# First mixer: the value projection moved from the end of the preceding head pair to the beginning of its own pair

## The chip, the core and the metric

The kernel runs on one core of a Trainium2 chip. Its engines have their own in-order queues and meet through semaphores: TensorE (PE) for matrix products and transposes, VectorE (DVE) and ScalarE (ACT) for elementwise work, GpSimd (POOL) and SyncE (SP), which here mostly issue transfers. The metric is the device time of one execution in microseconds; a smaller number is better.

## The reference

The reference is one step of a two-layer streaming encoder with model width 1024: a prompt of 1024 new frames and 8 running streams of 16 frames each, whose past of 1024 frames lies in caches. Layer 0 has a mixer with two halves, layer 1 a banded attention; each layer ends in an MLP. Only the first mixer matters here:

```
def ab_project(h, w_in):
    p = h @ w_in
    q, k, v, a, g = jnp.split(p, [...], axis=-1)
    return heads(q), heads(k), heads(v), a * jax.nn.sigmoid(g)

def stick_breaking(q, k, v, q_pos, k_pos):
    z = jnp.einsum('bqhd,bkhd->bhqk', q, k) * (HEAD_DIM ** -0.5)
    log_keep = jnp.where(mask, jax.nn.log_sigmoid(-z), 0.0)
    between = lax.cumsum(log_keep, axis=3, reverse=True) - log_keep
    w = jnp.where(mask, jnp.exp(jax.nn.log_sigmoid(z) + between), 0.0)
    return jnp.einsum('bhqk,bkhd->bqhd', w, v)

out = jnp.concatenate([a_out, c_out], axis=-1) @ w_out
```

There are 8 heads of 64, handled as four pairs of 128 columns. The other half of the mixer, `c_out`, is a causal depthwise convolution of width 31 over 512 channels of `a * sigmoid(g)`, followed by a layer norm and a SiLU. The new k and v of every head, and the last rows of the convolution's input, are outputs too.

## The kernel before, in words

**Tiles.** The 1024 prompt frames and the 8 x 16 sample frames form 1152 columns, in three groups of 384 (`G`, `NG`). A projection chunk makes 128 output columns of `w_in`: for each group it takes 24 matmuls of 128x384 (8 parts of the width, each as three products of the split halves), so 72 in all. These are `psp<-h,hl_wi`; in names such as `psp122` the digits are the head pair, the chunk (0 is q, 1 is k, 2 is v) and the group. `chunk_steps` makes the steps of a chunk, each step 12 matmuls.

**One head pair.** `expand_qk` copies q and k of the pair into the form that the score products take; half of it goes through transfers on POOL's queue (`k`, `l`). The scores `z` of a block of queries go to ACT (sigmoid) and DVE (the scan, `sg`), come back to PE for transposition (`tpa`) and for the product with the values (`ava`). The output goes as `cpa` to a DRAM tile, `cat_d`. The values take their own way: the third group is evacuated by ACT, the tile `sv` is written out by POOL, DVE then overwrites it in place with differences of neighbouring rows (`differences`), ACT negates the first column, and PE transposes it (`vt`, in `expand_v`). The differences overwrite what the write-out reads, so they wait for it to land. The running streams have steps of their own: key tiles `ct..k` come from the cache in blocks of 512 KB, three buffers in turn, and PE multiplies each with the queries (`zs`); then come `zn`, the softmax-like part, transposes (`st`, `sn`), products with cached values (`so`) and a last transposition (`sq`).

**The convolution.** Its 4 x 31 taps are pairs of DVE instructions (line 737) that have nothing to do with PE. `TAPS` says how many of the 124 are laid into the start and into head pairs 0, 1 and 2; what is left goes to pair 3. When a channel block has its last tap, its sum is put into `cat_d` (`cat_d<-u`), from where the layer norm (`conv_norm`: loads `yl`, mean product `mu`, ...) reads it in pair 3.

**Order.** Each piece of work is a `Step` with an estimated PE time, an estimated DVE time, a name, and optionally the name of a step it should follow and a lag. `merge` interleaves lists of steps so that each list progresses in proportion, and holds a step back until the modelled time of its predecessor plus the lag is over. `level` then spreads the taps by DVE time. The result is a fixed program order for all engines. In `mixer0` (lines 657 to 1018), before pair 0 all of chunk q, k and v of pair 0 are projected, with no other PE work between them. In pair p the lists are the attention steps with `expand_v` among the first, the stream's steps, the list `fill` with the projections for pair p + 1 (and, in pairs 0 and 1, the two chunks of the convolution's input for pair p + 2), and the taps. The weights of the chunks are loaded in a fixed sequence, each one chunk ahead, by SP.

**Pair 3** has no more projections. Its list `fill` holds the first half of the output projection instead: `ready_chunks` loads finished 128-column chunks of `cat_d` back (`cr`, on SP) and splits them into `cat`, and the products `psoa<-cat` follow. The tile of `cr` is that of `sk`, and one is in use at a time, so a chunk is loaded when the one before has been split.

Of the kernel before, what the change touches and what calls it, by code (L numbers as in the profile page):

```python
# [17 lines left out]
KC = 8  # L18
T = 1152
TP = 1024  # L20
TAPS = (26, 36, 38, 24)
G = 384
NG = 3
HD = 64
# [54 lines left out]
def level(steps, extra):  # L79


    pe, dve = sum(s.pe for s in steps), sum(s.dve for s in steps + extra)
    out, at, done, extra = [], 0.0, 0.0, list(extra)
    for s in steps:
        while extra and done + 0.5 * extra[0].dve < at / pe * dve:
            done += extra[0].dve
            out.append(extra.pop(0))
        out.append(s)
        at += s.pe
        done += s.dve  # L90
    return out + extra
# [7 lines left out]
def run(steps):  # L99
    for s in steps:  # L100
        s.go()
# [23 lines left out]
def tile_trunk(ctx, tc, ins, outs):  # L125
# [184 lines left out]
    def chunk_steps(n, got, ahead, h, ks, evac, name, depth=1, per=12):  # L310

        steps = [Step(0.0, lambda: [ahead(n + d) for d in range(depth + 1)], 1200.0)]
        for g in range(NG):
            box = {}

            def ps(g=g, box=box):
                if "p" not in box:
                    box["p"] = bank(f"ps{name}{g}")
                return box["p"]

            steps += dense(ps, lambda: got[n], h, g, ks, per)
            steps.append(Step(0.0, lambda g=g, ps=ps: evac(ps(), g), 470.0))
        return steps
# [333 lines left out]
    def mixer0():  # L657
        with ExitStack() as st:
# [8 lines left out]
            pp = Bufs(st.enter_context(pool("pair0")), ve=2)  # L667
# [77 lines left out]
            def ag(c):  # L745
                return (chunk_steps(at[16 + c], got, ahead, h, ks, lambda ps, g: gate(c, ps, g), f"g{c}")
                        + chunk_steps(at[12 + c], got, ahead, h, ks, lambda ps, g: value(c, ps, g), f"a{c}"))
# [121 lines left out]
                nc.vector.tensor_copy(unit, ident)  # L869


            def proj(p):
                steps = []
                for n, tag in enumerate(("sq", "sk", "sv")):
                    def evac(ps, g, n=n, tag=tag):
                        if g == 0:
                            S[tag, p] = pp.tile([P, T], F32, tag, f"{tag}0{p}")
                        if g < 2:
                            tt(S[tag, p][:, g * G:g * G + G], ps[:, :G], rstd[g], ALU.mult)
                        else:  # L880
                            ACT(S[tag, p][:, g * G:], ps[:, :G], AF.Copy)
                        if g == 2 and n:
                            put(outs["sb_k" if n == 1 else "sb_v"][p], S[tag, p])
                    steps += chunk_steps(at[4 * n + p], got, ahead, h, ks, evac, f"p{p}{n}")
                return steps

            def expand_qk(p):
                q, k = S["sq", p], S["sk", p]
                expand(qs, kd, kl, q, k)
                S["qn"] = pp.tile([P, P], F32, "qn", f"qn0{p}")  # L890
                S["kn"] = pp.tile([P, P], F32, "kn", f"kn0{p}")
                ACT(S["qn"], q[:, TP:], AF.Copy, scale=0.125)
                ACT(S["kn"], k[:, TP:], AF.Copy)
# [85 lines left out]
            start()  # L979
            qs, kd, kl = ([ep.tile([P, TP], F32R, f"{n}{i}", f"{n}{i}") for i in range(2)] for n in "qkl")  # L980
            vs = pp.tile([P, 8, 2, HD], F32, "vs", "vs0")
            run(level(proj(0), taps[:TAPS[0]]))
            taps = taps[TAPS[0]:]
            carry, cat_t = [], None
            for p in range(4):
                S["p"] = p
                expand_qk(p)
                if p < 3:
                    fill = proj(p + 1)
                    if p < 2:  # L990
                        fill[10:10] = ag(p + 2)
                    n = TAPS[p + 1]
                    mix, now, taps = [], taps[:n], taps[n:]
                else:
                    cat_t = new_hs("cat0")
                    (first, fill), now = part_out(0, range(3), pp, cat_t), []
                    for s in taps:
                        s.pe = 900.0
                    mix = taps + conv_norm(lambda: (conv_pool.close(), Bufs(st.enter_context(pool("ln")), t1=3, yl=5))[1],
                                           cat_t)  # L1000
                cat = Cat(0, p, wk, cat_t)
                jobs = attend(p, cat)
                body, left = pipeline(jobs[1:], jobs[0][2])
                steps = carry + [jobs[0][0]] + [Step(327.0, lambda p=p, g=g: expand_v(p, g)) for g in range(NG)]
                if p == 3:
                    late, = ready_chunks(0, [2], pp, cat_t)
                    late.name, late.after, late.lag = "ready", carry[-1].name, 3000.0
                    fill[0].after, fill[0].lag = "ready", 5000.0
                    fill = ready_chunks(0, range(2), pp, cat_t) + first + [late] + fill
                steps += [jobs[0][1]] + body  # L1010
                carry = left
                if p == 3:
                    steps += carry
                cs = sample_out(cat, wk, p)
                load = sample_caches(0, p, cp)
                sample = two_samples(*(sample_steps(0, p, bg, S, wk, load, soft, cs) for bg in range(2)))
                run(level(merge(steps, sample, fill, mix), now))
            return cat_t

# [68 lines left out]
    def part_out(layer, ks, pp, cat_t):  # L1088

        wo = ins["w_out_ab"] if layer == 0 else ins["w_out_c"]  # L1090
        got, ahead = weights_ahead([(wo[fc], ks) for fc in range(KC)], f"wo{layer}a")
        steps, xo = [], {}

        def old(fc):
            if fc < KC and fc not in xo:
                xo[fc] = pp.tile([P, T], F32, ("sq", "sv")[fc % 2], f"xo{layer}{fc}")
                if layer == 0:
                    dma(xo[fc].rearrange("p (g t) -> p g t", g=NG), ins["x"][:, :, fc, :].rearrange("g p t -> p g t"))
                else:
                    dma(xo[fc], x_d[:, fc, :])  # L1100

        for fc in range(KC):
            def evac(ps, g, fc=fc):
                xs = xo[fc][:, g * G:g * G + G]
                tt(xs, xs, ps[:, :G], ALU.add)
                if g == 2:
                    put(xm_d[layer][:, fc, :], xo[fc])
            steps.append(Step(0.0, lambda fc=fc: (old(fc), old(fc + 1))))
            steps += chunk_steps(fc, got, ahead, cat_t, ks, evac, f"oa{layer}{fc}", per=6)

        n = -(-len(SPLIT) * len(ks) // 6) + 1
        first = [steps[i] for i in (1, 2, 2 + n, 2 + 2 * n)]
        return first, [s for s in steps if s not in first]
# [872 lines left out]
```

## Time and profile before

| | |
|---|---|
| time, median of 3 runs | 2727.28 us (2727.0 to 2727.28) |
| the profiled execution | 2730.68 us |
| its span on the core | 2728.9 us |
| mean granted PE clock | 0.993 |
| PE busy | 2662.6 us, 98% |
| DVE busy | 2040.6 us, 75% |
| chunks before pair 0 (216 `psp` without a break) | 70.35 to 107.95 us |
| head pairs 0 to 2 | about 108 to 404 us |
| head pair 3 and its output projection | about 404 to 530 us |

A row of a timeline gives the start, the length of a run of like instructions on one engine, the line and operation, output<-inputs, the shape, the count, and in brackets the idle time of the engine ahead of it with what ended it. A row of windows gives, for a stretch of time, each engine's busy time with the number of instructions, then the granted PE clock, the DMA engines' busy share and the GB/s moved. A row of DMA issues gives output<-input, the issuing queue, the count, the size and the median us from issue to landing.

### The profile page before, as it was taken

The numbers are of one execution on the slowest core, as the hardware profiler recorded it, in microseconds if no ns is written. First come the engines' busy times: TensorE is split into PE (matmuls) and PEld (weight loads), VectorE is DVE, ScalarE is ACT, GpSimd is POOL, SyncE is SP. The second block draws the span as 40 slices with busy tenths as digits, with TensorE's granted clock in tenths as the row PEclk, the third lists the DMA queues.
The fourth block names the chain that finished last, engine by engine and source line by source line (L and its number), as shares of the span: only waits on it lengthen the run. The fifth ranks groups of instructions, "written<-read, shape, count | busy, mean of one in ns | idle before, by whom it ended". The sixth has DMA issues, their size and how long they took to land.

```text
span 2728.9 us, 50505 instructions
## 1 busy us (share of the span) xinstructions
PE 2662.6 (98%) x19362; PEld 2553.8 (94%) x19362; DVE 2040.6 (75%) x4105; ACT 1365.7 (50%) x2854; POOL 330.5 (12%) x599
## 2 busy tenths in 40 slices
PE   8999998999999999999999999998999999999998
PEld 8888886899999999999999999997999999999998
DVE  7999996787777755768577777778787777647577
ACT  5344456755555543445355555555455555534344
POOL 1000111131111100000011111110321111100001
PEclk9999999999999999999999999999999999999999
DMA  4344447443333486335444444446543334674344
GB/s 159 104 128 149 146 141 241 171 145 141 140 138 138 151 290 224 108 113 178 145 141 139 129 139 141 137 127 218 181 140 138 143 141 147 233 254 135 96 125 146
DMA packets 173203, 422.90 MB, mean 155 GB/s; under 512 B 25968, under 2 KB 53808, under 8 KB 170912
## 3 DMA queue, kind: packets, MB, share of 16 engines
q1 hardware_dynamic: 135696, 288.38, 32.6%
q0 software_dynamic: 37120, 131.27, 13.9%
q8 instruction: 152, 2.49, 0.4%
q14 instruction: 91, 0.75, 0.1%
q10 hardware_dynamic: 144, 0.02, 0.0%
HBM read 289.60 MB, written 117.34 MB: 149 GB/s over the span
## 4 chain that ended last, share of the span: by engine, by line
PE 84%; DVE 7%; ACT 3%; issue 3%; DMA 3%; POOL 0%; SPq 0%; DVEq 0%; ACTq 0%; POOLq 0%
PE pd L1705 26%; PE um L1480 25%; PE psc L225 10%; PE psp L225 4%; PE avc L469 2%; PE tpc L457 2%; PE psoa L225 2%; PE f L225 1%; PE zs L570 1%; PE zc L1220 1%; PE ava L398 1%; DVE y L737 1%; PE so L604 1%; PE psg L225 1%; PE psa L225 1%
## 5 line engine op out<-in xcount | busy, mean ns | idle before, releaser
L225 PE MATMUL psc<-h,hl_wc 128*128 128x384 f32 x1728 | 327.1, 339 | 0.0
L225 PEld LDWEIGHTS psc<-h,hl_wc 128*128 128x128 f32 x1728 | 296.8, 188 | 13.3 <-issue 10.9
L1480 PE MATMUL um<-sl,hl_m 128*128 128x288 f32 x1548 | 240.8, 296 | 0.0
L1480 PEld LDWEIGHTS um<-sl,hl_m 128*128 128x128 f32 x1548 | 218.2, 189 | 0.0
L1705 PE MATMUL pd<-tm,hl_wd 128*128 128x288 f32 x1584 | 214.7, 294 | 0.0
L1705 PEld LDWEIGHTS pd<-tm,hl_wd 128*128 128x128 f32 x1584 | 211.3, 189 | 0.0
L737 DVE SCALAR_TENSOR_TENSOR y<-u,dw,y 128x1024 f32<-128x1024 f32 (+1 forms) x232 | 177.5, 805 | 0.7
L1487 ACT ACTIVATE hdm<-hdm 128x288 f32<-128x288 f32 x192 | 84.7, 442 | 156.4 <-DVE hdm L1486 154.8
L225 PE MATMUL psp<-h,hl_wi 128*128 128x384 f32 x864 | 162.5, 340 | 0.0
L186 DVE TENSOR_TENSOR tm<-xr,tm 128x576 fp32r<-128x576 f32 (+1 forms) x120 | 85.7, 715 | 94.8 <-ACT tm L185 94.6
L225 PEld LDWEIGHTS psp<-h,hl_wi 128*128 128x128 f32 x864 | 148.4, 188 | 6.2 <-issue 5.1
L185 ACT ACTIVATE tm<-xr 128x576 fp32r<-128x576 f32 (+1 forms) x120 | 77.6, 647 | 94.7 <-PE pd L1705 75.9
L1480 PE MATMUL um<-sl,hl 128*128 128x288 f32 x756 | 119.1, 296 | 0.0
L1187 ACT ACTIVATE s<-s,mxc 128x640 f32<-128x640 f32 (+4 forms) x128 | 88.8, 694 | 60.2 <-DVE mxc L1184 58.6
L1705 PE MATMUL pd<-th,hl_wd 128*128 128x288 f32 x792 | 113.9, 297 | 3.8 <-DVE th L186 3.7
L1705 PEld LDWEIGHTS pd<-th,hl_wd 128*128 128x128 f32 x792 | 108.7, 191 | 4.5 <-DVE th L186 4.2
L1705 PE MATMUL pd<-xr,hl_wd 128*128 128x288 f32 x792 | 111.9, 295 | 0.0
L1705 PEld LDWEIGHTS pd<-xr,hl_wd 128*128 128x128 f32 x792 | 107.4, 189 | 0.0
L1480 PEld LDWEIGHTS um<-sl,hl 128*128 128x128 f32 x756 | 106.4, 188 | 0.8
L1705 PE MATMUL pd<-tm,hl 128*128 128x288 f32 x768 | 104.9, 295 | 0.0
L1705 PEld LDWEIGHTS pd<-tm,hl 128*128 128x128 f32 x768 | 103.1, 188 | 0.0
L185 ACT ACTIVATE whc<-tpc 128x512 fp32r<-128x512 f32 (+1 forms) x144 | 72.5, 523 | 46.7 <-PE tpc L457 45.7
(530 smaller groups left out, 6536.8 us busy)
## 6 DMA issues: line engine op xcount, KB each, us to landing
xr<-hb_d SPq DMA_DIRECT2D x208, 288.0 KB, 2.9
xr<-in_w_up_dram SPq DMA_DIRECT2D x64, 512.0 KB, 4.0
hb_d<-hdm POOLq DMA_DIRECT2D x96, 288.0 KB, 2.4
hb_d<-t POOLq DMA_DIRECT2D x96, 288.0 KB, 2.4
wm<-in_w_down_dram SPq DMA_DIRECT2D x64, 256.0 KB, 4.1
st_wd<-in_w_down_dram SPq DMA_DIRECT2D x64, 256.0 KB, 3.5
st_wc<-in_w_in_c_dram SPq DMA_DIRECT2D x44, 256.0 KB, 2.6
xm_d<-xo POOLq DMA_DIRECT2D x16, 576.0 KB, 3.8
```

The source lines that it names most:

```text
L185: ACT(hi, src, AF.Copy)
L186: return tt(lo, src, f(hi), ALU.subtract)
L225: mm(ps()[:, :G], hl[:, a, at:at + P], act[g][k // 4][b][:, k % 4, :], start=n == 0, stop=n == len(todo) - 1)
L398: mm(st["av"][64 * m:64 * m + 64, o0:o0 + n], vs[:, j, i], st["w"][gi][:, c0:c0 + n], start=gi == 0, stop=gi == last)
L457: nc.tensor.transpose(tp[:, c0 + q * P:c0 + (q + 1) * P], blocks.get(j, tile_q), ident)
L469: mm(st["av"][:, o0:o0 + n], vs[:, j, i].rearrange("p a d -> p (a d)"), src[:, c0:c0 + n], start=st["done"] == 0, stop=st["done"] == nmm - 1)
L570: mm(box["z"][at // 512][own, at % 512:at % 512 + kw], qb[:, own], k[:, b * kw:b * kw + kw], start=True, stop=True)
L737: stt(src if j == CW - 1 else dst, src, wj, dst, ALU.mult, ALU.add)
L1187: ACT(s[:, :n], s[:, :n], AF.Exp, bias=mx, scale=-1.0, accum_out=tot)
L1480: mm(banks[b, n][:, :TQ], w[:, a, c * P:c * P + P], combo(key, c)[:, h, n * TQ:n * TQ + TQ], start=k < 3 and c == 0 and i == 0, stop=c == ...
L1487: ACT(y, y, AF.Relu)
L1705: mm(ps, w[:, a, m * P:m * P + P], b[:, h, (n - ns[0]) * TQ:(n - ns[0]) * TQ + TQ], start=first and s == 0, stop=j == NJ - 1 and s == 2, s ...
```

## The change

Before pair 0 only q and k are projected. Each pair starts its `fill` with its own v, then projects q of the next pair, the convolution's input chunks (pairs 0 and 1) and k of the next pair. `expand_qk` becomes a step of its own, with lags behind it for the first score block and for the stream's queries; the transposes of v wait, in the model, for the end of the v chunk plus 3 us. In pair 3, v comes first in `fill`, then the two ready chunks and the output projection; the third chunk waits for the transposes of v. The taps are dealt 17, 40, 40, 27 where they were 26, 36, 38, 24. The sequence of the weight chunks does not change, nor does any instruction's work.

```diff
-TAPS = (26, 36, 38, 24)
+TAPS = (17, 40, 40, 27)
...
-            def proj(p):
+            def proj(p, *ns):
                 steps = []
-                for n, tag in enumerate(("sq", "sk", "sv")):
+                for n in ns:
+                    tag = ("sq", "sk", "sv")[n]
+
                     def evac(ps, g, n=n, tag=tag):
...
                     steps += chunk_steps(at[4 * n + p], got, ahead, h, ks, evac, f"p{p}{n}")
+                steps[-1].name = f"p{p}{ns[-1]}"
                 return steps
...
-            run(level(proj(0), taps[:TAPS[0]]))
+            run(level(proj(0, 0, 1), taps[:TAPS[0]]))
             taps = taps[TAPS[0]:]
             carry, cat_t = [], None
             for p in range(4):
                 S["p"] = p
-                expand_qk(p)
+                fill = proj(p, 2)
                 if p < 3:
-                    fill = proj(p + 1)
+                    fill += proj(p + 1, 0)
                     if p < 2:
-                        fill[10:10] = ag(p + 2)
+                        fill += ag(p + 2)
+                    fill += proj(p + 1, 1)
                     n = TAPS[p + 1]
                     mix, now, taps = [], taps[:n], taps[n:]
                 else:
                     cat_t = new_hs("cat0")
-                    (first, fill), now = part_out(0, range(3), pp, cat_t), []
+                    (first, later), now = part_out(0, range(3), pp, cat_t), []
...
                 body, left = pipeline(jobs[1:], jobs[0][2])
-                steps = carry + [jobs[0][0]] + [Step(327.0, lambda p=p, g=g: expand_v(p, g)) for g in range(NG)]
+                jobs[0][0].after, jobs[0][0].lag = f"x{p}", 6000.0
+                turned = [Step(327.0, lambda p=p, g=g: expand_v(p, g)) for g in range(NG)]
+                turned[0].after, turned[0].lag = f"p{p}2", 3000.0
+                turned[-1].name = f"v{p}"
+                steps = [Step(0.0, lambda p=p: expand_qk(p), 0.0, f"x{p}")] + carry + [*jobs[0][:2]] + turned + body
                 if p == 3:
                     late, = ready_chunks(0, [2], pp, cat_t)
-                    late.name, late.after, late.lag = "ready", carry[-1].name, 3000.0
-                    fill[0].after, fill[0].lag = "ready", 5000.0
-                    fill = ready_chunks(0, range(2), pp, cat_t) + first + [late] + fill
-                steps += [jobs[0][1]] + body
+                    late.name, late.after, late.lag = "ready", f"v{p}", 0.0
+                    later[0].after, later[0].lag = "ready", 5000.0
+                    fill += ready_chunks(0, range(2), pp, cat_t) + first + [late] + later
...
                 sample = two_samples(*(sample_steps(0, p, bg, S, wk, load, soft, cs) for bg in range(2)))
+                sample[0].after, sample[0].lag = f"x{p}", 8000.0
```

What this moves is seen in the program order. The first place is PE in pair 1, around the transposes of v (`vt010` to `vt012`). Before, the last v matmul (`psp122`) stands 78 rows ahead of the first transpose, with two groups of the next q between them:

```order
L225 MATMUL psp201_2310<-h0_71_191,hl_wi12_1_2015 128x384
L398 MATMUL ava013_2347<-wa0130_2234,vs0_747 64x256 x2
L398 MATMUL ava013_2347<-wa0131_2257,vs0_747 64x256 x2
L398 MATMUL ava013_2347<-wa0132_2264,vs0_747 64x256 x2
L398 MATMUL ava013_2347<-wa0133_2298,vs0_747 64x256
L398 MATMUL ava013_2347<-wa0133_2298,vs0_747 64x128
L943 MATMUL z1000_2366<-k0_743,q0_741 128x128
L944 MATMUL z1000_2366<-l0_745,q0_741 128x128
L946 MATMUL z1000_2366<-maskd_126,unit_127 128x128
L913 MATMUL vt010_2379<-ident_69,sv01_2071 128x128 x3
```

Now the last v matmul is followed by the 24 matmuls of one group of the next q (`psp200`) and then at once by the transposes. These are the last of the 24 and what follows:

```order
L225 MATMUL psp200_2340<-h0_61_187,hl_wi12_1_2122 128x384
L225 MATMUL psp200_2340<-h0_60_186,hl_wi12_1_2122 128x384
L225 MATMUL psp200_2340<-h0_71_191,hl_wi12_1_2122 128x384
L225 MATMUL psp200_2340<-h0_70_190,hl_wi12_1_2122 128x384
L916 MATMUL vt010_2374<-ident_69,sv01_2183 128x128 x3
L916 MATMUL vt011_2379<-ident_69,sv01_2183 128x128 x3
L916 MATMUL vt012_2386<-ident_69,sv01_2183 128x128 x3
L946 MATMUL z1020_2394<-k0_743,q0_741 128x384
```

In pair 0, 24 of these matmuls and four key tiles stand between (before: 24 matmuls), and in pair 2, 24 and three key tiles.

The second place is POOL's queue at the start of pair 3, ahead of the loads for the layer norm (`yl00` to `yl03`, which the products `mu` read). Before:

```order
L741 DMA cat_d0_109<-u3_2527 128x8x16
L883 DMA out_sb_v_dram<-sv03_4091 128x1152
L363 DMA cat_d0_109<-cs02_4012 128x128
L363 DMA cat_d0_109<-cpa212_4321 64x256
L352 DMA l1_746<-l1_746 64x1024
L1034 DMA yl00_4346<-cat_d0_109 128x384
L1034 DMA yl01_4347<-cat_d0_109 128x384
L1034 DMA yl02_4348<-cat_d0_109 128x384
L1034 DMA yl03_4349<-cat_d0_109 128x384
```

Now two more transfers of `expand_qk` stand between `cpa212` and the loads, and the write-out of v comes after them:

```order
L363 DMA cat_d0_109<-cpa212_4241 64x256
L352 DMA l0_745<-l0_745 64x1024
L349 DMA k1_744<-k1_744 64x1024
L352 DMA l1_746<-l1_746 64x1024
L1042 DMA yl00_4266<-cat_d0_109 128x384
L1042 DMA yl01_4267<-cat_d0_109 128x384
L1042 DMA yl02_4268<-cat_d0_109 128x384
L1042 DMA yl03_4269<-cat_d0_109 128x384
L1042 DMA yl10_4713<-cat_d0_109 128x384
L363 DMA cat_d0_109<-cpa213_4349 64x256
L885 DMA out_sb_v_dram<-sv03_4337 128x1152
```

On PE, `mu` now stands right behind the first group of v (`psp320`), where before it stood behind products of the first ready chunk. The third place is SP's queue in pair 3, which loads the ready chunks (`cr`), key tiles (`ct03k`), the weights of the output projection (`st_wo0a`) and the residual (`xo`). Before:

```order
L1081 DMA cr00_4356<-cat_d0_109 128x1152
L1098 DMA xo00_4607<-in_x_dram 128x3x384
L192 DMA st_wo0a5_0_5016<-in_w_out_ab_dram 128x384
L192 DMA st_wo0a6_0_5182<-in_w_out_ab_dram 128x384
L1081 DMA cr01_4373<-cat_d0_109 128x1152
L539 DMA ct03k03_4439<-in_sb_k_dram 128x4x256
L539 DMA ct03k10_4476<-in_sb_k_dram 128x4x256
```

Now five key tiles stand between the two ready chunks; `ct03k13` takes the buffer of `ct03k10`, which PE reads right after the last matmul of v(3):

```order
L1089 DMA cr00_4493<-cat_d0_109 128x1152
L539 DMA ct03k03_4379<-in_sb_k_dram 128x4x256
L539 DMA ct03k10_4385<-in_sb_k_dram 128x4x256
L539 DMA ct03k11_4417<-in_sb_k_dram 128x4x256
L539 DMA ct03k12_4515<-in_sb_k_dram 128x4x256
L539 DMA ct03k13_4524<-in_sb_k_dram 128x4x256
L1089 DMA cr01_4503<-cat_d0_109 128x1152
```

The products of the second chunk on PE stand two key tiles, one product of the layer norm and three products of the first chunk behind the last matmul of v(3); the transposes of v(3) follow them.

## The prediction

> **What bounds the kernel now.** I read the page first. TensorE (PE) is busy for 98% of the span and carries 84% of the chain that ended last, so a change that keeps the arithmetic can win only PE's idle time and the time PE runs at a lower clock.
>
> ```profile
> span 2728.9 us, 50505 instructions
> PE 2662.6 (98%) x19362; PEld 2553.8 (94%) x19362; DVE 2040.6 (75%) x4105; ACT 1365.7 (50%) x2854; POOL 330.5 (12%) x599
> PE 84%; DVE 7%; ACT 3%; issue 3%; DMA 3%; POOL 0%; SPq 0%; DVEq 0%; ACTq 0%; POOLq 0%
> ```
>
> The diff touches only the first mixer, from about 70 to 530 us. The table by windows (window, its length, then PE, PEld, DVE, ACT, POOL busy, clock, DMA share, GB/s) tells which engine sets the pace there.
>
> ```profile
> 70.00:108.00 38.00, 38.00 (x222) 38.00 (x221) 37.81 (x47) 9.08 (x16) 4.08 (x7) 1.00 0.29 75
> 108.00:404.00 296.00, 292.00 (x2224) 251.42 (x2223) 271.75 (x402) 139.93 (x331) 30.94 (x55) 0.99 0.45 139
> 300.00:480.00 180.00, 167.79 (x1288) 137.00 (x1283) 148.73 (x249) 105.04 (x240) 24.46 (x43) 0.98 0.60 193
> ```
>
> PE idles 4 us in the 296 us of the first three head pairs, and 12 us between 300 and 480, nearly all of it at the start of the last pair. DVE is full ahead of pair 0 (37.81 of 38.00) and has 24 us to spare in pairs 0 to 2. The timeline of PE names the holes (start, length, what, and in brackets the idle time ahead with what ended it):
>
> ```profile
> 70.35 37.60 PE L225 MATMUL psp<-h,hl_wi 128*128 128x384 f32 x216
> 107.79 0.22 PE L943 MATMUL z<-k,q 128*128 128x128 f32 x1
> 108.07 4.42 PE L225 MATMUL psp<-h,hl_wi 128*128 128x384 f32 x24
> 115.37 2.15 PE L913 MATMUL vt<-ident,sv 128*128 128x128 f32 x9 [2.88 <-ACT sv L904]
> 117.45 1.08 PE L570 MATMUL zs<-ct00k,qb 128*32 128x256 f32 x8
> ...
> 404.63 0.27 PE L612 MATMUL sq<-ident,sb 128*128 128x128 f32 x1
> 404.83 1.51 PE L398 MATMUL ava<-wa,vs 128*64 128x256 f32 x12
> 407.89 0.98 PE L388 MATMUL tpa<-ident,sg 128*128 128x128 f32 x7 [1.29 <-DVE sg L929]
> 414.60 0.69 PE L225 MATMUL psoa<-cat,hl_wo0a 128*128 128x384 f32 x1 [5.73 <-ACT cat L185]
> 419.66 2.85 PE L1040 MATMUL mu<-yl,ones 128*128 128x384 f32 x8
> 423.34 0.44 PE L225 MATMUL psoa<-cat,hl_wo0a 128*128 128x384 f32 x1 [0.83 <-ACT cat L185]
> 433.68 0.64 PE L570 MATMUL zs<-ct03k,qb 128*32 128x256 f32 x8 [1.30 <-ACT qb L561]
> 439.91 2.94 PE L225 MATMUL psoa<-cat,hl_wo0a 128*128 128x384 f32 x15 [1.44 <-ACT cat L185]
> ```
>
> A projection matmul takes 37.60/216 = 0.174 us, so one 72-matmul chunk is 12.5 us. The waits are 2.88 us for the value transposes `vt` of pair 0 and, in pair 3, 1.29 + 5.73 + 0.83 + 1.30 + 1.44; `mu`, 8 matmuls that need 8 x 0.174 = 1.4 us, took 2.85 and so hides 1.5 more. The granted clock (seventh entry after the window's length) adds to this:
>
> ```profile
> 112.00:115.00 3.00, 0.49 (x3) 0.17 (x1) 3.00 (x5) 0.00 (x0) 0.00 (x0) 0.94 0.35 126
> 115.00:118.00 3.00, 2.63 (x17) 1.98 (x17) 2.85 (x3) 1.62 (x5) 0.00 (x0) 0.50 0.00 0
> 118.00:122.00 4.00, 4.00 (x26) 2.61 (x19) 2.14 (x4) 2.01 (x5) 0.00 (x0) 0.57 0.48 150
> 415.00:418.00 3.00, 3.00 (x18) 2.05 (x17) 2.21 (x4) 1.51 (x4) 0.37 (x1) 0.50 1.13 297
> 418.00:421.00 3.00, 3.00 (x21) 1.50 (x16) 0.00 (x0) 1.13 (x3) 0.00 (x0) 0.93 1.03 384
> ```
>
> Behind the 2.88 us wait PE runs at 0.50 and 0.57: 2.63 x 0.50 + 4.00 x 0.43 = 3.0 us lost. Behind the 5.73 us wait it is 3.00 x 0.50 + 3.00 x 0.07 = 1.7.
>
> **The change part by part.** Work stays the same; 12.5 us of projection moves from before pair 0 to pair 3, and what stands between v and `vt` becomes short in each pair. So the chain v to `vt` decides. In pair 0 it reads:
>
> ```profile
> 107.99 0.49 ACT L881 ACTIVATE sv<-psp 128x384 f32<-128x384 f32 x1 [1.45 <-PE psp L225]
> 108.77 0.56 POOL L883 DMA_DIRECT2D out_sb_v_dram<-sv  x1 [3.92 <-ACT sv L881]
> 113.78 1.21 DVE L903 TENSOR_TENSOR sv<-sv 128x1023 f32<-128x1023 f32 x1
> ...
> out_sb_v_dram<-sv POOLq DMA_DIRECT2D x1, 576.0 KB, 4.0
> out_sb_v_dram<-sv POOLq DMA_DIRECT2D x1, 576.0 KB, 5.9
> ```
>
> The last matmul ends at 107.95; evacuation, write-out to HBM, and only when that has landed the differences in place, then the transposes: 0.8 to the put, 4.0 landing, 1.2 differences, 0.4 for the ACT fix and the start, 6.4 us in all. With the 5.9 us landing of pair 1 it is 8.3.
>
> *Pair 0.* Cover after v: three key tiles (8 matmuls 0.64 each), 0.4 of `zn`, 24 psp (4.2), a fourth key tile: 7.1 us. ACT also has the softmax between, so I leave 0.6 us of wait (0 to 2). Gain: 2.88 + 3.0 - 0.6 = **-5.3**.
>
> *Pair 1.* Only 24 psp (4.2 us) stand between the last v matmul and `vt`: a new wait of 6.4 - 4.2 = 2.2 to 8.3 - 4.2 = 4.1; I take the middle, **+3.1**; the queries, `z` and psp of pair 1 are queued behind it. The nearest wait, 2.88, cost 3.0 of clock; a shorter one may cost none, so the bounds are 0 and 3.0 and I take **+1.5**.
>
> *Pair 2.* 24 psp and three key tiles, 6.1 us of cover: 0.3 to 2.2, I take **+1.0**.
>
> *Key tiles of the running streams.* Three buffers, so a fourth tile is asked for only when the first is used:
>
> ```profile
> ct00k<-in_sb_k_dram SPq DMA_DIRECT2D x3, 512.0 KB, 3.8
> ct01k<-in_sb_k_dram SPq DMA_DIRECT2D x5, 512.0 KB, 4.6
> ```
>
> In the new order the fourth comes about 3.9 to 4.6 us after the first, against 0.4 to issue and 3.8 to 4.6 to land: 0 to 1 us in each of pairs 0 to 2. I take **+1.0** for the three.
>
> *Taps.* One tap is a pair of DVE instructions, 177.5/116 = 1.53 us:
>
> ```profile
> L737 DVE SCALAR_TENSOR_TENSOR y<-u,dw,y 128x1024 f32<-128x1024 f32 (+1 forms) x232 | 177.5, 805 | 0.7
> 190.00:200.00 10.00, 10.00 (x87) 8.82 (x86) 10.00 (x15) 5.21 (x11) 1.11 (x2) 1.00 0.45 159
> ```
>
> Nine taps leave the start and come into pairs 0 to 2 (+4, +2, +3): 13.8 us. DVE had 24.3 to spare there, so 10.5 remain, hidden on average; but in 190 to 200 DVE is already full, and work added in such a stretch is late for PE. Bounds 0 and 4 (a quarter of 13.8); I take **+1.0**.
>
> *Pair 3.* Call K the last matmul of k(3). Before, v(3) followed and attention steps and chunk products ran while DMAs landed; now PE passes `sq`, `ava`, 15 transposes and 24 psp to `mu`: 0.2 + 1.5 + 15 x 0.98/7 + 4.2 = K + 8.0. The loads of `yl` are issued on POOL, whose queue is in order:
>
> ```profile
> 409.89 0.55 POOL L363 DMA_DIRECT2D cat_d<-cpa  x1 [0.96 <-DVE cpa L412]
> 410.97 0.58 POOL L1034 DMA_DIRECT2D yl<-cat_d  x1
> 412.81 1.60 POOL L1034 DMA_DIRECT2D yl<-cat_d  x3 [1.26 <-DMA cat_d<-u]
> yl<-cat_d POOLq DMA_DIRECT2D x5, 192.0 KB, 6.4
> cr<-cat_d SPq DMA_DIRECT2D x3, 576.0 KB, 6.6
> 404.62 0.34 SPq L1081 DMA_DIRECT2D cr<-cat_d  x1
> 416.11 0.33 SPq L1081 DMA_DIRECT2D cr<-cat_d  x1
> ```
>
> Before, the first `yl` load went out 410.97 - 404.63 = 6.3 us after the same `sq`. Now two more puts (k1, l1) of 0.55 stand ahead: K + 7.4. Landing took 6.4, so the first is there at K + 13.8 and the fourth, 1.6 us of issues later, at K + 15.4. PE waits 15.4 - 8.0 less 0.5 for the three earlier `mu` products, 6.9; with 4.6 us of landing, as the key tiles took, 5.1. I take **6.2**, nearer the former since it is the row of these very loads, and **1.7** of clock as behind the 5.73. Queued behind `mu` on PE are the remaining 48 psp of v(3) and so all of pair 3.
>
> The second chunk, cr01, moves behind five key tiles on SP, the last of which needs the buffer that PE frees just after v(3) ends (V + 0.6). So it goes out at V + 1.1, lands 6.6 later, and with ACT 0.5 and DVE 0.5 its product can start at V + 8.7. PE is there at V + 2.2 (two key tiles, 0.4 of `rr`, three products): **6.5** idle (5.8 with the 5.9 us of landing above, 7.7 with DVE first at the differences), and **1.7** of clock. `vt` follows it and is covered. The other waits I leave at 0.5. After: 6.2 + 1.7 + 6.5 + 1.7 + 0.5 = 16.6. Before: 1.29 + 5.73 + 1.7 + 1.5 + 0.83 + 1.30 + 1.44 = 13.8. **+2.8**; with the lower ends 5.1 and 5.8 it is +0.5, with the upper ends, 3.0 of clock each and 1.5 of other waits, +8.3.
>
> **Sum**: -5.3 + 3.1 + 1.5 + 1.0 + 1.0 + 1.0 + 2.8 = +5.1 us on the profiled execution's 2730.68, which is 3.4 above the median 2727.28; carried to the median, **2732.4**. A measurement of this kernel tells 0.2% (5.45 us) from no change, so this is at the edge of that, on the slow side.
>
> [...]
>
> **Rivals.**
> *A, the covers hold (faster).* cr01 comes in time because PE, held at `mu`, lets the chunk's inputs land meanwhile: its 6.5 + 1.7 falls away. `vt` waits at the low bounds (0, 2.2 without clock, 0.3), key tiles and taps nothing: -5.9 + 2.2 + 0.3 + 2.8 - 8.2 = -8.8, **2718.5**. For it: before, cr00 took 404.62 to 414.03 under saturated DMA, and now less is in flight. Against: cr01's place behind key tiles that wait for PE.
> *B, the write-out of v sets every pair (slower).* If landings are 5.9 us as in pair 1, `vt` waits 4.1 in pair 1 and 2.2 in pair 2, each with 3.0 of half clock: -5.3 + 7.1 + 5.2 + 1.0 + 1.0 + 2.8 = +11.8, **2739.1**. It decides from a landing of about 5.5 us. Against it: 4.0 and 3.9 in pairs 0 and 2.
> *C, DVE becomes the bound (slower).* If half of the 13.8 us of taps falls where DVE is full, 6.9 replaces 1.0: +11.0, **2738.3**. Against it: 24 us to spare.
>
> **How the numbers follow.** Forecast 0.45: all its lower ends together give -2.9, 2724, all the upper ones +20.7, 2748; its own range is 2725 to 2739. Rival A 0.30 (2711 to 2724), B 0.12, C 0.10, the page's rule 0.03. Faster: 0.26 of A and 0.02 of the forecast, 0.28. Same: 0.24 + 0.04 of A + 0.03 of B and C, 0.31. Slower: 0.19 of the forecast, 0.11 of B, 0.08 of C, 0.03, 0.41. The likeliest time is 2732; the range runs from 2714 to 2743, into A and past B and C.
>
> **What would show it.** `vt` of pair 0 with under 1 us of wait and no half clock behind; `vt` of pair 1 waiting 2 to 4 us on the differences; PE waiting about 6 us at the first `mu` on `yl`, then about 6 at the second chunk's product on `cat`; DVE near full from 108 to 404. It is wrong if `mu` or that product comes without a wait (A), if `vt` of pair 2 waits 2 us or more with a half clock (B), or if psp or `z` wait on DVE for several us in pairs 0 to 2 (C).

## The result, and the profile after

The changed kernel takes 2740.11 us (median of 5 runs, 2737.16 to 2740.5) against 2727.28 us (2724.68 to 2731.47): a ratio of 1.0044, 95% interval 1.0034 to 1.0055, so 12 us slower (9 to 15). Its profiled execution has a span of 2738.3 us. In the timeline of PE of the changed kernel, the rows with the larger waits between 100 and 450 us are these; the columns are those of the timeline shown for before:

```profile
114.88 0.64 PE L570 MATMUL zs<-ct00k,qb 128*32 128x256 f32 x8 [2.19 <-DMA ct00k<-in_sb_k_dram]
117.50 1.20 PE L916 MATMUL vt<-ident,sv 128*128 128x128 f32 x9 [0.54 <-ACT sv L907]
220.81 0.64 PE L570 MATMUL zs<-ct01k,qb 128*32 128x256 f32 x8 [2.72 <-DMA ct01k<-in_sb_k_dram]
229.79 2.18 PE L916 MATMUL vt<-ident,sv 128*128 128x128 f32 x9 [3.09 <-ACT sv L907]
337.84 0.64 PE L570 MATMUL zs<-ct02k,qb 128*32 128x256 f32 x8 [1.86 <-ACT qb L561]
412.74 5.01 PE L1048 MATMUL mu<-yl,ones 128*128 128x384 f32 x8 [7.24 <-DMA yl<-cat_d]
435.23 0.91 PE L285 MATMUL rr_l<-sq_l,ones 128*128 128x384 f32 x2 [2.04 <-DVE sq_l L281]
441.64 1.60 PE L225 MATMUL psoa<-cat,hl_wo0a 128*128 128x384 f32 x3 [4.98 <-ACT cat L185]
```

The wait of 2.88 us at `vt` of pair 0 is gone, but 2.19 at the fourth key tile and 0.54 at `vt` stand in its place. Pair 1, which had no wait, now has two, 5.8 us together; pair 2, which had one of 0.91 at `tpa`, has 1.86 at the streams' queries. In pair 3, 1.29 + 5.73 + 0.83 + 1.30 + 1.44 of waits became 7.24 + 2.04 + 4.98. The windows of the changed kernel (length, then busy times of PE, PEld, DVE, ACT, POOL, granted clock, DMA share, GB/s) show the pairs as a whole and the stretches at a lower clock:

```profile
70.35:103.00 32.65, 32.65 (x191) 32.65 (x190) 32.46 (x41) 8.44 (x14) 4.09 (x7) 1.00 0.29 78
103.00:400.00 297.00, 285.63 (x2198) 246.03 (x2197) 275.53 (x408) 140.47 (x333) 30.29 (x52) 0.99 0.46 141
114.00:118.00 4.00, 2.58 (x20) 1.85 (x21) 3.59 (x4) 1.80 (x5) 0.00 (x0) 1.00 1.03 338
229.00:233.00 4.00, 3.21 (x15) 3.14 (x15) 3.88 (x6) 1.99 (x6) 0.00 (x0) 0.57 0.01 4
338.00:342.00 4.00, 4.00 (x24) 2.33 (x17) 4.00 (x5) 0.68 (x5) 0.00 (x0) 0.58 0.92 319
412.00:417.00 5.00, 4.26 (x7) 2.45 (x8) 0.00 (x0) 0.00 (x0) 0.00 (x0) 0.50 0.36 128
441.00:448.00 7.00, 6.36 (x24) 5.77 (x25) 4.01 (x8) 5.32 (x13) 0.55 (x1) 0.51 0.51 155
```

In pairs 0 to 2 PE is idle 11.4 us of 297 where it was idle 4.0 of 296. The clock stays at 1.00 behind the waits of pair 0 and falls behind those of pairs 1, 2 and 3: 3.21 x 0.43 + 4.00 x 0.42 + 4.26 x 0.50 + 6.36 x 0.49 = 8.3 us lost, against 3.0 + 1.7 before. DVE is nearly full ahead of pair 0 as before, and has 21.5 us to spare behind it.

### The profile page after: what moved, and what is told of

Read it like the earlier page. It is cut to its first block, busy times and chain, and to the rows that moved or that the text cites. A ratio compares the mean times of both kernels' runs of the same rounds, so it can differ in the third digit from the quotient of the medians.

```text
span 2738.3 us, 50481 instructions
## 1 busy us (share of the span) xinstructions
PE 2661.5 (97%) x19362; PEld 2555.4 (93%) x19362; DVE 2039.2 (74%) x4105; ACT 1364.8 (50%) x2854; POOL 329.5 (12%) x599
## 4 chain that ended last, share of the span: by engine, by line
PE 71%; DVE 4%; ACT 2%; DMA 1%; issue 1%; DVEq 0%; ACTq 0%; SPq 0%
PE pd L1713 26%; PE um L1488 25%; PE psc L225 10%; PE avc L469 2%; PE tpc L457 2%; PE zc L1228 1%; PE zc L1229 1%; PE psoa L225 1%; PE so L604 1%; PE zs L570 1%; PE psob L225 0%; DMA cr<-cat_d 0%; DVE xr L1394 0%; ACT s L1195 0%; DMA lo<-in_w_down_dram 0%
## 5 line engine op out<-in xcount | busy, mean ns | idle before, releaser
L225 PEld LDWEIGHTS psc<-h,hl_wc 128*128 128x128 f32 x1728 | 296.8, 188 | 13.3 <-issue 10.9
```

Of the source, the lines that this page charges most:

```text
L225: mm(ps()[:, :G], hl[:, a, at:at + P], act[g][k // 4][b][:, k % 4, :], start=n == 0, stop=n == len(todo) - 1)
```

## The experiments

Each time is a median with the ratio to the kernel before, run on the same chip, and its 95% interval. The changed kernel stands at 1.0044.

**Pair 3 as it was.** v(3) is projected at the end of pair 2, and pair 3 gets its old order; pairs 0 to 2 start as in the changed kernel.

```diff
-                fill = proj(p, 2)
+                fill = proj(p, 2) if p < 3 else []
...
                     fill += proj(p + 1, 1)
+                    if p == 2:
+                        fill += proj(3, 2)
...
```

> Pairs 0 to 2 start as in the changed kernel, but v(3) is projected at the end of pair 2 and pair 3 has its old order. Theory S (the loss is the sum of waits behind four short covers, each with its clock): in the changed kernel pair 3 waits 7.2 at mu, 2.0 at rr_l, 5.0 at the second chunk and 1.7 later, with 5.3 of clock, against 13.3 of waits, 1.9 of clock and 1.5 hidden before, so this version gives back 5 to 7 us: 2733 to 2735. Rival P (all of the loss is in pair 3): 2727 or less, since pair 0 gained. Rival D (the taps make DVE the bound): no change, 2740.

Measured: 2730.83 us, 1.0017 (1.0008 to 1.0026). Pair 3 accounts for 1.0044 - 1.0017, 0.27% or 7.4 us; the other three pairs together for 0.17%, 4.6 us. By the intervals of the ratios, the first is known to about 4 us, the second to 2.5. Rivals P and D fall: pairs 0 to 2 are a loss too, and undoing pair 3 alone with the new taps helps. The time is a little better than S gave.

**The old deal of the taps** in the changed order. The first tap of the last channel block here comes ahead of the last group's product with `a`, so it works on unmultiplied values of that group; the amount of work is the same.

```diff
-TAPS = (17, 40, 40, 27)
+TAPS = (26, 36, 38, 24)
```

> The changed order with the old deal of the taps, 26, 36, 38, 24. Theory S: pairs 0 to 2 gain nothing from 9 fewer taps (13.8 us of DVE), since PE waited only 0.5 us for DVE there; the start, now 33 us and full on DVE, gets 13.8 us more than it can hold, so that q and k of pair 0 come late: 5 to 12 us slower than the changed kernel, 2745 to 2752. Rival D: with the taps taken out of pairs 0 to 2 the kernel gets faster, 2735 or less.

Measured: 2747.87 us, 1.0074 (1.0060 to 1.0088), 8 us slower than the changed kernel. In the timeline of its PE, `vt` of pair 0 waits 10.58 us:

```profile
123.68 2.18 PE L916 MATMUL vt<-ident,sv 128*128 128x128 f32 x9 [10.58 <-ACT sv L907]
```

With 12.5 us of projection taken from the start, 26 taps no longer fit there, so the nine taps had to move. What they cost in their new place this run can't tell, since it adds a cost of its own at the start.

**`vt` later.** The stream's product with its own new v stands ahead of `vt` in the order here and so takes the preceding pair's values.

```diff
-                turned[0].after, turned[0].lag = f"p{p}2", 3000.0
+                turned[0].after, turned[0].lag = f"p{p}2", 9000.0
```

> The lag ahead of the transposes of v goes from 3 to 9 us, so that 24 to 40 more projection matmuls and key tiles stand between v and vt in pairs 0 to 2. Theory S: the wait of vt in pair 1 (3.1 us) and the 0.5 in pair 0 go, and 1.5 us of half clock with them; the fourth key tile and pair 3 keep theirs: 5 us less, 2735. Rival W (the wait moves to the next user, the products ava or the scores): 2739 to 2741, with a new wait of 2 us or more on ava in pair 1.

Measured: 2733.24 us, 1.0021 (1.0012 to 1.0030): 6 us of the 12. `vt` waits nowhere in pairs 0 to 2. The largest new wait there is 1.09 us at `ava`, in pair 2, so W falls. The gain is not from `vt` alone, and for the most part not from there: up to the end of k(3) PE's idle time fell only from 10.9 to 8.6 us, while in pair 3 `mu` waited 0.85 + 1.36 in place of 7.24, and `vt` of pair 3 came up with 3.65.

**`mu` later.**

```diff
-                     Step(2600.0, centre, 1900.0, f"c{name}", f"l{name}", 4000), ...
+                     Step(2600.0, centre, 1900.0, f"c{name}", f"l{name}", 12000 if g == 0 else 4000), ...
```

> The lag ahead of the first mean product mu in pair 3 goes from 4 to 12 us. In the order it then stands behind the second group of v, and cr01 goes out on SP ahead of ct03k03 rather than behind ct03k13. Theory S: PE is at mu about K + 17, the fourth yl was due at K + 15.4, so its 7.2 us go with 2.2 of clock, and the second chunk's 5.0 us with 3.1 of clock shrink to 0 to 2: 2740 less 12 to 17, 2723 to 2728. Rival L (pair 3 is held by its transfers, and what PE saves it waits later, at vt, rr_l, the third chunk or the residual): 2735 or more.

Measured: 2734.17 us, 1.0028 (1.0017 to 1.0038). PE reaches `mu` at 417.65 and waits for nothing, and the wait of the second chunk is gone. The rows of the timelines of PE, POOL and DVE show what came up instead:

```profile
417.65 2.85 PE L1048 MATMUL mu<-yl,ones 128*128 128x384 f32 x8
433.43 2.18 PE L916 MATMUL vt<-ident,sv 128*128 128x128 f32 x9 [6.07 <-ACT sv L907]
426.62 0.57 POOL L885 DMA_DIRECT2D out_sb_v_dram<-sv  x1 [10.91 <-ACT sv L883]
431.92 1.22 DVE L906 TENSOR_TENSOR sv<-sv 128x1023 f32<-128x1023 f32 x1 [1.72 <-DMA out_sb_v_dram<-sv]
```

By the ratios 4 us came, by the medians 6, of the 12 that S expected at least; the rest is at `vt` of pair 3, which had been hidden behind the second chunk's wait and is now the last to be ready: written out at 426.62, differences at 431.92, `vt` at 433.43. That is rival L, in part.

**v(0) alone** moved to its own pair.

```diff
-                fill = proj(p, 2)
+                fill = proj(0, 2) if p == 0 else []
...
-                    fill += proj(p + 1, 1)
+                    fill += proj(p + 1, 1) + proj(p + 1, 2)
...
-TAPS = (17, 40, 40, 27)
+TAPS = (17, 45, 38, 24)
```

> Only v(0) goes into its own pair; pairs 1 to 3 keep the old order with v at the end of the pair before; 17 taps at the start, 45 in pair 0. Theory S: pair 0 keeps a wait of 2.2 to 2.7 us at the fourth key tile in place of 2.9 at vt, without the 3.0 of half clock behind it, and nothing new comes up later: 2727 less 3, 2724. Rival D (nine more taps in pair 0 are late for PE): 2728 or more, with waits on DVE.

Measured: 2726.02 us, 1.0000 (0.9992 to 1.0009). Its pair 0 looks like that of the changed kernel, 2.00 us at the fourth key tile, 0.54 at `vt` and no half clock (1.00 in every microsecond from 70 to 165), and the waits for DVE are the same two, 0.90 and 1.29, as before. In its timeline of PE:

```profile
113.87 0.64 PE L570 MATMUL zs<-ct00k,qb 128*32 128x256 f32 x8 [2.00 <-DMA ct00k<-in_sb_k_dram]
116.49 1.20 PE L916 MATMUL vt<-ident,sv 128*128 128x128 f32 x9 [0.54 <-ACT sv L907]
```

That its median shows no gain means that this form of pair 0 is worth less than the 5.9 us that one profile of before showed: its waits, 2.54, are nearly as long as the 2.88 they replace. What became of the half clock stays open. It may not come in every execution of before, or come in others of this version; that is argued, not shown.

**Key tiles apart.**

```diff
-                + [Step(1300.0 * nz / nk, lambda c=c: keys(c), 0.0, None, f"q{name}", 3000) for c in range(nk)],
+                + [Step(1300.0 * nz / nk, lambda c=c: keys(c), 0.0, f"k{name}{c}", f"q{name}" if c < 3 else f"k{name}{c - 3}",
+                        3000 if c < 3 else 6500) for c in range(nk)],
```

> The changed kernel with the fourth key tile of each stream group held 6.5 us behind the first, so that 24 projection matmuls stand between them. Theory S: the waits of 2.2 and 2.7 us at the fourth key tile in pairs 0 and 1 go, the waits of vt (now with a key tile ahead of it) stay: 2740 less 3 to 5, 2735 to 2737. Rival V (the time only goes to the wait of vt next to it, which ends when the write-out has landed): 2739 to 2741.

Measured: 2739.56 us, 1.0052 (1.0040 to 1.0065), no better than the changed kernel. The wait at the fourth key tile is down to 1.36 us in pair 0 and gone in pair 1, and `vt` has taken it over in pairs 1 and 2, as the timeline of its PE shows:

```profile
224.41 1.54 PE L917 MATMUL vt<-ident,sv 128*128 128x128 f32 x6 [4.79 <-ACT sv L908]
335.63 0.87 PE L917 MATMUL vt<-ident,sv 128*128 128x128 f32 x6 [3.87 <-ACT sv L908]
```

Rival V. The wait of the key tile had been covering part of the wait of `vt`: the two are not terms of a sum.

**All lags together**, with the key tiles apart and `mu` later as above, and the stream's product with the new v held behind `vt` (`merge` also waits for the step named in `also`).

```diff
-                turned[0].after, turned[0].lag = f"p{p}2", 3000.0
+                turned[0].after, turned[0].lag = f"p{p}2", 7000.0 if p < 3 else 9000.0
...
+                for s in sample:
+                    if s.name == f"o0{p}00":
+                        s.also = f"v{p}"
```

> All three lags together in the changed order: vt 7 us behind v (9 in pair 3), key tiles apart, mu 12 us behind its loads; the streams' product with their new v waits for vt in the order. Theory S: the waits of pairs 0 to 2 shrink from 10 us to 2 or 3 and their clock from 3 to 0 to 2, pair 3 has mu and the second chunk covered and vt(3) behind nine more products: 2740 less 16 to 24, 2716 to 2724, faster than both. Rival L (pair 3 is bound by what it must load after v(3), and waits at the third chunk or the residual in their place): 2725 to 2732.

Measured: 2732.91 us, 1.0033 (1.0021 to 1.0046), above even rival L's range. In pairs 1 and 2 `vt` still waits 3.89 and 4.13 us, though 7 us of lag stand ahead of it; in pair 3 the third chunk waits 3.70, `st` 3.31 and `so` 2.12.

**Pairs 0 to 2 spread out, pair 3 old.** Pair 3 is as in the first version above; pairs 0 to 2 have `vt` 7 us behind v, the key tiles apart, and the stream's product behind `vt`.

> Pairs 0 to 2 with v in their own pair, vt 7 us behind v and key tiles apart; pair 3 in its old order, with v(3) projected in pair 2. Theory S: pair 3 costs what it cost before, pairs 0 to 2 lose their waits and the 2.9 + 3.0 of before as well: 2727 less 4 to 6, 2721 to 2723. Rival D (13.8 us more DVE work in pairs 0 to 2 is late for PE when the other waits no longer cover it): 2726 or more.

Measured: 2722.57 us, 0.9991 (0.9982 to 1.0000). One wait is left in pairs 0 to 2, 3.89 us at `vt` of pair 1. PE has 9.5 us of other work between v and `vt` there, yet the chain takes longer (timelines of POOL, DVE and PE around it, and the issue to landing):

```profile
216.74 0.12 POOL L697 MEMSET u<- 128x30 f32 x1 [4.26 <-DMA cat_d<-u]
217.80 0.58 POOL L886 DMA_DIRECT2D out_sb_v_dram<-sv  x1
224.26 1.27 DVE L738 SCALAR_TENSOR_TENSOR y<-u,dw,y 128x1024 f32<-128x1024 f32 x1
225.46 1.35 DVE L932 TENSOR_TENSOR_SCAN kps<-kps 128x576 f32<-128x576 f32 x1
226.72 0.33 DVE L738 SCALAR_TENSOR_TENSOR y<-u,dw,y 128x128 f32<-128x128 f32 x1
226.97 0.76 DVE L933 TENSOR_TENSOR kps<-kps 128x575 f32<-128x575 f32 x1
227.63 1.22 DVE L907 TENSOR_TENSOR sv<-sv 128x1023 f32<-128x1023 f32 x1
229.15 1.45 PE L917 MATMUL vt<-ident,sv 128*128 128x128 f32 x9 [3.89 <-ACT sv L908]
...
out_sb_v_dram<-sv POOLq DMA_DIRECT2D x1, 576.0 KB, 6.5
```

The write-out was issued at 217.80 and had landed at 224.3, but the differences start at 227.63: a tap, the softmax's scan and its product stand ahead of them on DVE. `expand_v` issues the differences in the step that also issues the first transposes, so whoever moves `vt` back on PE moves the differences back on DVE by as much, and they can meet DVE's backlog anew.

**The differences as a step of their own**, 5.5 us behind v, and `vt` 3.5 us behind them in pairs 0 to 2, on the version just shown.

```diff
-                turned[0].after, turned[0].lag = f"p{p}2", 7000.0 if p < 3 else 3000.0
+                d, t = ((5500.0, 3500.0) if p < 3 else (0.0, 0.0))
+                turned.insert(0, Step(0.0, lambda p=p: differences(p), 1300.0, f"d{p}", f"p{p}2", d))
+                turned[1].after, turned[1].lag = f"d{p}", t
...
-                if g == 0:
-                    differences(p)
```

> The version with pairs 0 to 2 spread out and the old pair 3 (2722.6), with the differences of v as a step of their own 5.5 us behind v, and vt 3.5 us behind them. There vt of pair 1 still waited 3.9 us, with 1.7 of clock, since the differences stand on DVE where vt stands on PE, behind taps and the softmax. Theory Q (DVE's queue, not the landing, sets vt once the cover is long): the differences run 3 us earlier, the wait goes, 4 to 5 us less, 2717 to 2719. Rival B (the landing of the write-out, 6.5 us there, sets it): DVE now waits for the landing with its taps behind it, and the time stays at 2721 to 2724.

Measured: 2720.11 us, 0.9973 (0.9963 to 0.9983), faster than both kernels. By the timelines of DVE and PE the differences of pair 1 now start at 223.71 and `vt` waits for nothing:

```profile
223.71 1.23 DVE L907 TENSOR_TENSOR sv<-sv 128x1023 f32<-128x1023 f32 x1
224.84 1.36 DVE L930 TENSOR_TENSOR_SCAN kps<-kps 128x576 f32<-128x576 f32 x1
226.32 1.20 PE L915 MATMUL vt<-ident,sv 128*128 128x128 f32 x9
```

So Theory Q holds for this wait: the differences follow the operation ahead of them on DVE, which ends at 223.81, without a gap, and so did not wait for the landing, which had taken 6.5 us in the other version. How long it took here is not shown. The size is less sure. The step from 0.9991 to 0.9973 is 4.9 us, as Q gave, by the medians it is 2.5, and the two intervals just meet. The trace gives about 2: other waits came up elsewhere, the two longest of them these,

```profile
150.72 0.55 PE L388 MATMUL tpa<-ident,sg 128*128 128x128 f32 x3 [0.99 <-ACT sg L949]
237.63 0.39 PE L945 MATMUL z<-k,q 128*128 128x256 f32 x1 [1.27 <-DVE cpa L412]
```

so that PE's idle time up to the end of k(3) fell only from 4.2 to 3.9 us. What went with the long wait is its 1.7 us of half clock: the mean granted clock from 103 to 400 us is 1.00 here.

**The same on the version with all lags** and the changed pair 3 (there the differences stand 7 us behind v, and `vt` 4 us behind them).

> The version with all lags and the changed pair 3 (2732.9), with the differences as a step of their own. Theory Q: the waits of vt in pairs 1 and 2 (3.9 and 4.1, with 1.7 and 2.8 of clock) go, pair 3 keeps its waits at the third chunk (3.7), st (3.3) and so (2.1): 8 to 11 us less, 2722 to 2725, still not under the version with the old pair 3. Rival B: 2730 or more.

Measured: 2725.43 us, 0.9993 (0.9983 to 1.0002), 11 us less than without it by the ratios and 8 by the medians, as Q gave. Here the trace agrees: up to the end of k(3) PE's idle time fell from 9.5 to 6.2 us, and of the half clock, 1.7 + 2.8 us, the part in pair 2 went (1.00 from 265 to 358 us); the mean granted clock of the profiled execution rose from 0.992 to 0.995. From the version with the old pair 3, timed beside it, 5 us separate it; its PE still has two waits in pair 3:

```profile
419.72 2.06 PE L225 MATMUL psoa<-cat,hl_wo0a 128*128 128x384 f32 x5 [4.32 <-ACT cat L185]
432.31 1.11 PE L590 MATMUL st<-ident,sgs 128*128 128x128 f32 x4 [3.20 <-ACT vs L917]
```

**The same as the only edit** of the changed kernel, in pairs 0 to 2; in pair 3 the differences come at once behind v, and `vt` 3 us behind them.

> The changed kernel with nothing but the differences as a step of their own in pairs 0 to 2, 5.5 us behind v, and vt 3.5 us behind them (9 in all); the product with the new v waits for vt. Pair 3 and the key tiles as in the changed kernel. Theory Q: vt waits nowhere in pairs 0 to 2, the key tiles keep their 2 to 3 us in each pair with some clock, pair 3 keeps mu, rr_l and the second chunk: 2740 less 4 to 6, 2734 to 2736. Rival V (what vt no longer waits, the key tiles or the products wait): 2738 or more.

Measured: 2733.17 us, 1.0024 (1.0015 to 1.0033), 0.20% below the changed kernel, and as good as `vt` later by its lag alone. Here too `mu` waits only 1.07 + 1.36, and the key tiles and the queries keep 2.06, 3.04 and 2.27. By its time rival V is out, but not by the place of the gain: up to the end of k(3) PE's idle time fell only from 10.9 to 9.7 us, though `vt` no longer waits its 0.54 + 3.09, and the larger part came in pair 3 and its output projection, 16.4 to 12.3. In pairs 0 to 2 other waits did take over most of what `vt` gave up.

**The kernel before, with the differences of pair 0 as a step of their own**, and nothing moved but that, `vt` of pair 0 and, in every pair, the stream's product with the new v, which waits for `vt`.

```diff
+                if p == 0:
+                    jobs[0][0].name = "s0"
+                    turned[0].after, turned[0].lag = "d0", 3500.0
+                    steps[1:1] = [Step(0.0, lambda p=p: differences(p), 1300.0, "d0", "s0", 4500.0)]
```

> The kernel before, with nothing moved but the start of pair 0: the differences of v(0) are a step of their own 4.5 us behind the first scores, and vt of pair 0 stands 24 matmuls and three key tiles further back. If the wait of vt and the half clock behind it (2.9 + 3.0 in the profile of before) can be had by itself: 2.9 to 5.9 us less than before, ratio 0.9978 to 0.9989. Rival N (the pair 0 wait is worth little, as in the version with v(0) alone moved, whose ratio was 1.000, since the clock dip does not come in every execution and DVE is full there): 0.9990 to 1.0010.

Measured: 2722.32 us, 0.9982 (0.9973 to 0.9991): 5 us (2.5 to 7); by the medians 3.3. In the timeline of its PE `vt` of pair 0 comes without a wait:

```profile
114.66 1.14 PE L913 MATMUL vt<-ident,sv 128*128 128x128 f32 x9
```

So the wait at pair 0 can be had without moving a projection at all, and its interval overlaps that of the best version here. Rival N, whose range ends at 0.9990, falls but for the edge of the interval, and with it the reading that the wait of pair 0 is worth nothing. Where 2.5 us of other waits replaced it, nothing was gained; here only 1.05 us came up, at `vt` of pair 1, the clock stood at 1.00 from 70 to 165 and from 265 to 358 us, and the gain is about 5.

## Why the prediction was right or wrong

**The direction and the range.** The forecast was a small loss at the edge of what can be measured, 2732; the loss is clear, 2740, inside the range. Of the three outcomes, slower had the largest chance, 0.41. The signs named for it came: `vt` of pair 0 at 0.54 us without half clock, `vt` of pair 1 at 3.09 on the differences, `mu` and the second chunk at 7.24 and 4.98, and DVE busy for 274 of 296 us. So the direction was not luck; the range, 29 us wide, would have held a gain too. The point was 8 us too low: pairs 0 to 2 were given +2.3 and cost 4.6, pair 3 was given +2.8 and cost 7.4. By steps:

**Pair 0 (-5.3).** In the profile, the old wait and its half clock went, as said, and `vt` waited 0.54 for the 0.6 that was left. What took the gain back is the fourth key tile ahead of `vt`: it was booked as cover, and is itself late by 2.19, which belongs to the key tiles' term below. Moving v(0) alone gave no gain in the median. That the 2.88 + 3.0 was there to be had, or most of it, is what the kernel before with only pair 0's differences moved shows, with its 5 us.

**vt of pair 1 (+3.1, clock +1.5).** The wait was 3.09 and the clock lost 3.21 x 0.43 = 1.4. The sizes agree, but only in part the mechanism: the landing was 3.9 us, the short end, and the rest came from engines in between. The last v matmul ended at 222.2; of ACT, POOL and DVE, and of the issues to landing:

```profile
223.51 0.49 ACT L883 ACTIVATE sv<-psp 128x384 f32<-128x384 f32 x1
224.30 0.58 POOL L885 DMA_DIRECT2D out_sb_v_dram<-sv  x1 [0.27 <-ACT sv L883]
227.00 1.35 DVE L979 TENSOR_TENSOR sgs<-sgs,kps 128x1151 f32<-128x1151 f32 x1
228.28 1.23 DVE L906 TENSOR_TENSOR sv<-sv 128x1023 f32<-128x1023 f32 x1
229.53 0.20 ACT L907 ACTIVATE sv<-sv 128x1 f32<-128x1 f32 x1 [4.07 <-DVE sv L906]
...
ct01k<-in_sb_k_dram SPq DMA_DIRECT2D x4, 512.0 KB, 6.3
out_sb_v_dram<-sv POOLq DMA_DIRECT2D x1, 576.0 KB, 3.9
```

The evacuation was 1.3 us late behind the softmax of the key tile that PE had waited for. The write-out had landed at 228.2, just when DVE, which had been busy without a break, came to the differences; a quicker landing alone would have gained nothing.

**vt of pair 2 (+1.0).** It did not wait. A wait of 1.86 for the streams' queries came ahead of it, and the clock behind that cost 4.00 x 0.42 = 1.7; neither was in the sum.

**Key tiles (+1.0).** This is the first term that failed: 2.19 + 2.72 in pairs 0 and 1. The landing was taken as 3.8 to 4.6 from rows of before; in the changed order the four tiles of pair 1 took 6.3 (median), and the two that PE waited for 5.0 in pair 0 and 5.8 in pair 1. The cover was short as well: PE was at the fourth tile of pair 0 at 112.69, 2.8 us after it was asked for at 109.86. Spreading them showed that the wait is not a term of its own either, since `vt` took it over.

**Taps (+1.0).** Only 0.48 us of waits directly for DVE came up ahead of pair 3, and the old deal was slower, not faster. As the bound on PE by itself, rival C is out. But DVE's order, which the prediction treated as spare time, set the differences wherever the cover was made long enough.

**Pair 3 (+2.8).** This is the largest error: 7.4 us by the version that puts pair 3 back. One of its terms was misread: the 2.85 us of `mu` hid no wait of 1.5 before. `mu` takes the same 2.85 at full clock where nothing waits, as the row at 417.65 above shows (granted clock 1.00 from 415 to 425 us there); its eight matmuls took 0.36 us each, where `psp` took 0.174. Without that 1.5 on the side of before the term is +4.3, and the forecast 2733.9. `mu` waited 7.24 for 6.2. PE reached it at 412.74 - 7.24 = 405.5, 8.4 us behind K at 397.1 (8.0 was said), and the loads were issued at 404.31, 7.2 us behind K (7.4); what was under-sized is the landing (timelines of POOL and SP, and the issues to landing):

```profile
404.31 1.68 POOL L1042 DMA_DIRECT2D yl<-cat_d  x3
406.44 1.07 POOL L1042 DMA_DIRECT2D yl<-cat_d  x2 [0.45 <-DMA k<-k]
403.89 0.34 SPq L1089 DMA_DIRECT2D cr<-cat_d  x1
433.50 0.34 SPq L1089 DMA_DIRECT2D cr<-cat_d  x1
yl<-cat_d POOLq DMA_DIRECT2D x5, 192.0 KB, 8.2
```

The row of before had 6.4. The second chunk went out at 433.50, 1.4 us behind v(3), as said, and its wait was 4.98 for 6.5, partly because `rr_l`, which the sum did not hold, waited 2.04 in front of it. The clock was lost for 4.26 x 0.50 + 6.36 x 0.49 = 5.2, where 3.4 was taken. Rival A, that the wait at `mu` would let cr01 arrive in time, is refuted by the row of 433.50: its place behind the key tiles held it back.

**Rival B**, that the write-out sets every pair, gave 2739 and lies near the time, by luck and not for its own reason: the landing of v was not late in pair 1, 3.9 us, and pair 2 did not wait for v. **The chance of 0.03** stands for a rule that no run shows. The traces showed half clock behind 2.88 us before and behind 3.09 and 1.86 us in the changed kernel, and none behind 2.19 and 2.72.

## What to carry to other kernels

When a producer is moved closer to its consumer, count every engine between them, and each one's place in its own queue; here the transfer was 3.9 us of 7.6. An operation that shares a step with its consumer moves with it, so a longer lag can buy less than it seems: with 7 us of lag and the key tiles apart `vt` still waited 3.89, and issued apart it did not. With 9 us it did not wait either, so the lag is not useless. In pair 0 the wait went without moving the large piece of work at all. Waits next to each other cover one another: before pricing one at what it shows, ask which is due next behind it.

## What the runs showed of the hardware

The clock fell behind some waits and not behind others. In the changed kernel it fell behind 1.86 us in pair 2 and stayed at 1.00 behind 2.19 and 0.54 in pair 0; before, it fell behind 2.88. The traces of before and of the changed kernel show a pattern in it. Between 60 and 560 us their stretches at half clock last 3.41, 6.83 or 10.24 us, and within each trace they begin whole multiples of 3.41 us apart: at 114.62 and 411.58 before, at 229.43, 338.66, 410.34 and 437.64 in the changed kernel. Three pairs of neighbouring windows of the changed kernel, cut at these multiples (the columns as above), for pairs 0, 1 and 2:

```profile
113.38:116.80 3.42, 1.92 (x15) 1.35 (x15) 3.01 (x4) 1.19 (x3) 0.00 (x0) 1.00 1.03 345
116.80:120.21 3.41, 2.87 (x27) 2.40 (x30) 2.77 (x4) 2.74 (x10) 0.00 (x0) 1.00 0.87 283
226.02:229.43 3.41, 0.68 (x4) 0.36 (x3) 3.41 (x5) 0.00 (x0) 0.00 (x0) 1.00 0.65 235
229.43:232.84 3.41, 3.05 (x14) 3.05 (x15) 3.41 (x6) 1.83 (x6) 0.00 (x0) 0.50 0.00 0
335.24:338.66 3.42, 1.55 (x14) 0.82 (x13) 3.42 (x5) 3.32 (x12) 0.57 (x1) 1.00 0.92 291
338.66:342.07 3.41, 3.41 (x16) 2.15 (x16) 3.41 (x5) 0.15 (x2) 0.00 (x0) 0.50 0.90 299
```

The waits of pair 0 are split by the borders, 1.50 us of idle time in the window with the most, and the clock stays. In pairs 1 and 2 one window holds 2.73 and 1.87 us, and the next runs at half. Cut so between 60 and 560 us, the two traces have 278 windows at full clock with another behind them: each of the six with 1.87 us or more of idle time is followed by one at half clock, none of the 272 with 1.66 or less is. The borders lie elsewhere in the two traces, since 229.43 - 114.62 is 33.6 times 3.41 us. That the same wait can cost clock in one execution and not in another is the author's estimate from this; each kernel has one trace here. The loss comes in like portions, 1.4 us in pair 1 and 1.7 in pair 2, with 3.0 where two windows follow, as in pair 0 of before.

For pricing, the waits of 1.9 to 3.1 us in pairs 0 to 2 of these two traces cost themselves plus 0 or 1.4 to 3.0 us of clock. So a loss seen in a single profile is rather an upper end than an expectation; that too is an estimate.
